# Filler weights and stores issued from GpSimd's queue, the product weights from SP's

## The chip, the cores and the metric

The kernel runs on one core of a Trainium2 chip. The metric is the device time of one execution in microseconds, the median over runs of the same program. A core has five engines that run side by side, each through its own instruction list in the order in which that list was written: TensorE (PE in the profile, its weight loads PEld), VectorE (DVE), ScalarE (ACT), GpSimd (POOL) and SyncE (SP). Transfers between HBM and the on-chip memory are started by an instruction on one of the engines' lists and then run on the DMA engines. Such an instruction waits, like any other, until its semaphores allow it, and what stands behind it on its list waits with it. "The queue" of an engine means here the DMA instructions on its list.

## The reference

Two layers (DEPTH = 2) of a hybrid mixer, on 128 context rows and 512 latent rows of width 2048. Cut to what matters here:

```python
def layer_step(x, cvec, p, rope, attend, s0_f, s0_b):
    norm_g, w_ada, b_ada, w_in, qg, kg, lb, hg, lng, lnb, ws, bs, w_out = p
    shift, scale, gate = adaln(cvec, w_ada, b_ada)      # silu(cvec) @ w_ada + b_ada, three parts of 2048
    h = rms_norm(x, norm_g) * (1.0 + scale) + shift
    aq, ak, av, ag, bq, bff, bfb, bi, bg, cu, cv, cg = split_proj(h @ w_in)   # 2048 x 6656
    q, k, v = qkv_heads(aq, ak, av, qg, kg, rope)
    a_out = attend(q, k, v) * jax.nn.silu(ag)
    b_out, s_f, s_b = hgrn_mixer(bq, bff, bfb, bi, bg, lb, hg, s0_f, s0_b)
    c_out = sgu_mixer(cu, cv, cg, lng, lnb, ws, bs)
    y = jnp.concatenate([a_out, b_out, c_out], axis=-1) @ w_out               # 2048 x 2048
    return x + gate * y, k, v, s_f, s_b
```

Outputs are the two streams after both layers, and for each layer the context's keys and values (`ck`, `cv`) and the final states of the recurrence (`st`).

## The kernel before, in words

All 640 rows (five tiles t of 128) go through the same weights. A product with `w_in` or `w_out` is made either as `rowmajor` (512 columns at a time, 16 steps k over the 2048 rows of the weight, five row tiles into five PSUM banks) or as `colmajor` (128 columns at a time, four loads of four k each). For every k, or every four k, one weight tile `wr` of 256 KB is loaded (`wraw`, line 635, pool `wrp` of 4 buffers), ACT rounds it to `wh` (line 643), DVE makes the rest `wl = wr - wh` (line 644; both in pool `whp`, 3 buffers each), and PE multiplies `wh` and `wl` with the two halves `hh` and `hl` of the activations: lines 655 to 657 (three matmuls for each of the five t, 15 for a `wr`) or line 663. In `rowmajor` the last two k share their five t.

The adaLN vectors that are not needed at once are made beside the products by a *filler*: `ada_gen` walks through blocks of 512 columns of `w_ada`, `ada_steps` makes one block. A block is 16 steps k: load a tile `wa` of 128x512 (256 KB, line 296, pool `arp` of 2 buffers), then two DVE instructions that add it, times the conditioning value of context and of latent rows, to the accumulator `aacc` (line 300 for k = 0, line 302 after it). Two more steps end a block with a few matmuls. `aacc` has one buffer. The filler gets `fill_rate` steps after each group of matmuls: 0.85 during layer 0's projections, 1.25 during its `out_proj`, 0.5 in layer 1. There are 12 blocks in layer 0 and 4 in layer 1, 256 `wa` loads in all. The first blocks of adaLN, the context projections and the first norm of layer 0 have loads of their own (`rows_block` line 264, `first_round` lines 410 and 426), which the change does not touch.

`out_proj` (line 1240 on) runs `w_out` in four passes of 512 columns, c = 0 to 3. After each pass DVE multiplies the five PSUM tiles by the gate (line 1264) and adds the residual (line 1266), and the result is stored: in layer 0 to a scratch `x1` (line 1271), in layer 1 to the outputs (line 1269). Other stores: `ck` and `cv` in `k_prep` (lines 826 and 827), `st` in `hgrn` (line 1080).

The order within an engine's list is made by a scheduler when the program is built, from the program's order, priorities and buffers that come free. A block `with self.hi():` lifts what is in it by 3000 places: loads of `wr` and `wa` are put where their buffers come free. The list of each engine is then fixed.

Of the kernel before, what the change touches and what calls it, by code (L numbers as in the profile page):

```python
# [18 lines left out]
P = 128  # L19
# [56 lines left out]
class Net:  # L76
# [213 lines left out]
    def ada_steps(self, l, blk):  # L290
        nc = self.nc
        acc = self.sml.tile([P, 2, 512], F32, tag="aacc", name=self.nm("aacc"), bufs=1)
        for k in range(KT):
            with self.hi():
                r = self.arp.tile([P, 512], F32, tag="ar", name=self.nm("wa"))
                nc.sync.dma_start(r, self.I["w_ada"][l, k * P:(k + 1) * P, 512 * blk:512 * blk + 512])
            for cd in range(2):
                sc = self.s2[:, k, cd:cd + 1]
                if k == 0:
                    nc.vector.tensor_scalar(acc[:, cd], r, sc, None, op0=ALU.mult)  # L300
                else:
                    nc.vector.scalar_tensor_tensor(acc[:, cd], r, sc, acc[:, cd], op0=ALU.mult, op1=ALU.add)  # L302
            yield
        yield
        b = self.bank()
        if blk >= 8:
            for cd in range(2):
                nc.tensor.matmul(b[32 * cd:32 * cd + 32, :], lhsT=self.ones[:, 0:32], rhs=acc[:, cd], start=True, stop=True,
                                 skip_group_check=True)
            rows = self.g(512)  # L310
            br = self.g(512)
            nc.scalar.dma_start(br[0:64], self.I["b_ada"][l, 512 * blk:512 * blk + 512].partition_broadcast(64))
            nc.vector.tensor_tensor(rows[0:64], b[0:64], br[0:64], op=ALU.add)
            c0 = 512 * (blk - 8)
            nc.scalar.dma_start(self.gd[l][:, c0:c0 + 512], rows[0:64:32])
        else:
            for i in range(4):
                for cd in range(2):
                    nc.tensor.matmul(b[:, 2 * i + cd:2 * i + cd + 1], lhsT=acc[:, cd, i * P:(i + 1) * P],  # L319
                                     rhs=self.ones[:, 0:1], start=True, stop=True, skip_group_check=True)  # L320
            self.mod_cols(l, blk // 4, 4 * (blk % 4), 4, b[:, 0:8].rearrange("p (s c) -> p s c", c=2))
        yield
# [489 lines left out]
    def k_prep(self, l):  # L812
        nc, O = self.nc, self.O
        ks = self.kss
        nc.scalar.activation(ks, ks, AF.Ln, bias=self.bias[:, 0:1], scale=1.0 / P)
        nc.scalar.activation(ks, ks, AF.Exp, scale=-0.5)
        for t in range(NT):
            kr = self.kraw[t]
            for gi in range(2):
                sl = slice(gi * P, gi * P + P)  # L820
                nc.vector.scalar_tensor_tensor(kr[:, sl], kr[:, sl], ks[:, 2 * t + gi:2 * t + gi + 1],
                                               self.gqk[:, 1], op0=ALU.mult, op1=ALU.mult)
            src = kr[:, 0:256]
            if t == 0:
                for gi in range(2):
                    nc.sync.dma_start(O["ck"][0, l, gi], kr[:, gi * P:gi * P + P])
                    nc.sync.dma_start(O["cv"][0, l, gi], self.vprm(gi))
            else:
                t1 = self.g(512)
                self.rope_ap(src, t, 2, t1[:, 0:256], t1[:, 256:512], t1[:, 0:256])  # L830
                src = t1[:, 0:256]
                yield
                yield
            b = self.bank()
            for gi in range(2):
                nc.tensor.transpose(b[:, gi * P:(gi + 1) * P], src[:, gi * P:(gi + 1) * P], self.ident)
            for gi in range(2):
                self.put_k(gi, b, None if t == 0 else self.KPOS[t])
            yield
# [211 lines left out]
    def hgrn(self, l, h, es, q):  # L1051
        nc, I, O = self.nc, self.I, self.O
# [8 lines left out]
        for d in range(2):  # L1061
            nc.sync.dma_start(S[d][:, 0], I["state_hgrn"][0, l, d, h])
            pre.append(self.hgrn_prep(l, h, d, es[d], q))
            for _ in range(8):
                yield
            kd = pre[d][5]
            kT = self.g(512)
            b = self.bank()
            for n in range(4):
                j = order[d][n]  # L1070
                nc.tensor.transpose(b[:, n * P:(n + 1) * P], kd[:, j * P:(j + 1) * P], self.ident)
            nc.scalar.activation(kT, b, AF.Copy)
            yield
            U = self.bank()
            for n in range(4):
                nc.tensor.matmul(U[:, n * P:(n + 1) * P], lhsT=kT[:, n * P:(n + 1) * P], rhs=vj[order[d][n]],
                                 start=True, stop=True, skip_group_check=True)
            So = self.sml.tile([P, P], F32, tag="So", name=self.nm("So"), bufs=2)
            nc.scalar.activation(So, U[:, 0:P], AF.Copy)
            nc.sync.dma_start(O["st"][0, l, d, h], So)  # L1080
            for n in range(1, 4):
                nc.vector.scalar_tensor_tensor(S[d][:, n], S[d][:, n - 1], pre[d][4][:, order[d][n], 4:5],
                                               U[:, n * P:(n + 1) * P], op0=ALU.mult, op1=ALU.add)
# [63 lines left out]
        for j in range(NT):  # L1147
            dst = b1[:, j * P:(j + 1) * P] if j < 4 else b2[:, 0:P]
# [90 lines left out]
    def out_proj(self, l):  # L1239
        nc, I, O = self.nc, self.I, self.O  # L1240
        last = l == DEPTH - 1
        xt = []
        for t in range(NT):
            with self.hi():
                x = self.mg()
                if l == 0:
                    src = I["x_prompt"][0] if t == 0 else I["x_sample"][0, (t - 1) * P:t * P]
                else:
                    src = self.x1[t]
                nc.scalar.dma_start(x[:, 0:D], src)  # L1250
            xt.append(x)
        ssq = self.small(4 * NT, "ssq")
        for c in range(4):
            cs = slice(512 * c, 512 * c + 512)
            gb = []
            for cd in range(2):
                gt = self.g(512)
                nc.scalar.dma_start(gt, self.gd[l][cd, cs].partition_broadcast(P))
                gb.append(gt)
            ps = self.rowmajor(I["w_out"][l], 512 * c)  # L1260
            for t in range(NT):
                with self.hi():
                    y = self.ev(512)
                    nc.vector.tensor_tensor(y, ps[t], gb[0 if t == 0 else 1], op=ALU.mult)
                xs = xt[t][:, cs]
                nc.vector.tensor_tensor(xs, xs, y, op=ALU.add)
                if last:
                    dst = O["yp"][0] if t == 0 else O["ys"][0, (t - 1) * P:t * P]
                    nc.sync.dma_start(dst[:, cs], xs)
                else:  # L1270
                    nc.sync.dma_start(self.x1[t][:, cs], xs)
                    junk = self.g(512)
                    nc.scalar.activation(junk, xs, AF.Square, accum_out=ssq[:, 4 * t + c:4 * t + c + 1])
        self.xt, self.ssq = xt, ssq
# [149 lines left out]
```

## Time and profile before

| | before |
|---|---|
| median of 3 runs | 2294.43 us (2293.33 to 2295.41) |
| the profiled execution's own time | 2299.35 us |
| its span, first to last instruction | 2297.6 us |
| mean granted TensorE clock | 0.994 |
| PE busy | 2241.8 us, 98% of the span |
| DVE, ACT, POOL busy | 1379.9, 940.4, 0.7 us |
| DMA engines' mean busy share, SP's and ACT's queues (q1 and q10 of the page are theirs) | 38.1% + 3.4% |

How to read it: a row of the waits names the engine and line that stood idle, what released it, the total in us, how often, and the longest. "SPq" is SP's list of DMA instructions. Matmuls are pipelined: a record of 0.39 us stands every 0.23 us where PE is not held up, so busy time of PE is not the same as PE at its full rate. A row of a table of windows gives, for a stretch in us from the span's start, its length, busy time and count of instructions, the granted clock, the share of the DMA engines and GB/s.

### The profile page before, as it was taken

What the parts mean: (1) busy time and instruction counts of PE and PEld (TensorE: products, weight loads), DVE (VectorE), ACT (ScalarE), POOL (GpSimd) and SP (SyncE); (2) the same over time, 40 slices, a digit from 0 to 9 for tenths busy, and PEclk for the clock granted to TensorE, in tenths of its full rate; (3) what the DMA queues carried; (4) which work ended last, traced back from release to release, by engine and by line L of the source; (5) the groups of instructions that cost most, each with busy time, mean ns of one, the idle gap of its engine ahead of it and who ended that gap; (6) DMA issues with size and microseconds to landing.
All of it is one profiled execution on the core that took longest, in us unless ns stands there. A gap on an engine that the chain in (4) does not pass through costs nothing.

```text
span 2297.6 us, 35103 instructions
## 1 busy us (share of the span) xinstructions
PE 2241.8 (98%) x13248; PEld 1943.6 (85%) x13248; DVE 1379.9 (60%) x2655; ACT 940.4 (41%) x2289; POOL 0.7 (0%) x8
## 2 busy tenths in 40 slices
PE   5999999999999999999989999999999999999999
PEld 3766678899999998978877887799999999898887
DVE  5436878648578675776668555744845644254332
ACT  4323455544554662422224246453635445233111
POOL 0000000000000000000000000000000000000000
PEclk9999999999999999999999999999999999999999
DMA  9675634334344354465553321422423322326332
GB/s 326 223 256 191 208 95 127 108 91 126 111 123 122 91 162 127 134 216 186 178 189 92 103 63 49 126 61 78 143 72 100 114 70 76 97 70 205 112 108 79
DMA packets 266031, 299.05 MB, mean 130 GB/s; under 512 B 17507, under 2 KB 166901, under 8 KB 264069
## 3 DMA queue, kind: packets, MB, share of 16 engines
q1 hardware_dynamic: 254368, 271.27, 38.1%
q10 hardware_dynamic: 11492, 25.53, 3.4%
q8 instruction: 104, 1.70, 0.3%
q14 instruction: 67, 0.54, 0.1%
HBM read 281.69 MB, written 15.04 MB: 129 GB/s over the span
## 4 chain that ended last, share of the span: by engine, by line
PE 82%; DVE 7%; DMA 6%; ACT 1%; issue 1%; DVEq 0%; SPq 0%; ACTq 0%
PE m L663 34%; PE m L655 12%; PE m L657 12%; PE m L656 12%; DMA wa<-in_w_ada_dram 5%; DVE aacc L302 2%; PE s L240 2%; PE s L898 2%; DVE wl L644 1%; PE s L944 1%; PE s L1111 1%; PE s L956 1%; PE s L1126 1%; PE s L957 1%; PE s L319 1%
## 5 line engine op out<-in xcount | busy, mean ns | idle before, releaser
L644 DVE TENSOR_TENSOR wl<-wr,wh 128x512 fp32r<-128x512 f32 (+1 forms) x535 | 367.1, 688 | 561.6 <-ACT wh L643 560.4
L643 ACT ACTIVATE wh<-wr 128x512 fp32r<-128x512 f32 (+1 forms) x535 | 336.0, 629 | 884.7 <-PE m L657 533.0
L655 PE MATMUL m<-wh,hh 128*128 128x512 f32 x1440 | 571.5, 397 | 2.7 <-ACT hh L385 2.7
L656 PE MATMUL m<-wl,hh 128*128 128x512 f32 x1440 | 568.6, 395 | 5.7 <-DVE wl L644 5.5
L657 PE MATMUL m<-wh,hl 128*128 128x512 f32 x1440 | 566.1, 394 | 0.0
L663 PE MATMUL m<-hh,wh 128*128 128x384 f32 x2016 | 477.9, 317 | 0.0
L663 PE MATMUL m<-hh,wl 128*128 128x384 f32 x2016 | 466.0, 310 | 0.0
L663 PE MATMUL m<-hl,wh 128*128 128x384 f32 x2016 | 465.8, 310 | 0.0
L302 DVE SCALAR_TENSOR_TENSOR aacc<-wa,s,aacc 128x512 f32<-128x512 f32 x480 | 344.1, 747 | 78.8 <-DMA wa<-in_w_ada_dram 77.4
L655 PEld LDWEIGHTS m<-wh,hh 128*128 128x128 f32 x1440 | 272.3, 189 | 75.4 <-issue 10.3
L656 PEld LDWEIGHTS m<-wl,hh 128*128 128x128 f32 x1440 | 272.5, 189 | 63.9 <-DVE wl L644 9.7
L657 PEld LDWEIGHTS m<-wh,hl 128*128 128x128 f32 x1440 | 272.2, 189 | 60.2 <-issue 4.7
L663 PEld LDWEIGHTS m<-hh,wh 128*128 128x128 f32 x2016 | 309.9, 188 | 14.8 <-issue 9.8
L663 PEld LDWEIGHTS m<-hh,wl 128*128 128x128 f32 x2016 | 310.0, 188 | 2.0 <-issue 1.8
L663 PEld LDWEIGHTS m<-hl,wh 128*128 128x128 f32 x2016 | 310.0, 188 | 1.9 <-issue 1.4
L1097 ACT ACTIVATE mg<-ev,Dt 128x32 f32<-128x32 f32 x480 | 113.4, 309 | 10.3 <-PE s L1111 10.1
L948 DVE TENSOR_TENSOR g<-s,g 128x512 fp32r<-128x512 f32 x56 | 38.5, 690 | 37.8 <-ACT g L947 29.9
L928 ACT ACTIVATE g<-g,st,qs 128x384 f32<-128x384 f32 (+1 forms) x64 | 48.0, 752 | 31.0 <-DVE st L924 31.0
L944 PE MATMUL s<-misc,g 128*128 128x128 f32 x240 | 45.9, 285 | 4.4 <-ACT g L933 4.0
L933 ACT ACTIVATE g<-g,st 128x384 f32<-128x384 f32 (+2 forms) x80 | 43.8, 605 | 10.9 <-DVE st L931 10.9
L898 PE MATMUL s<-kT,g 128*128 128x256 f32 (+1 forms) x288 | 46.7, 304 | 0.0
L902 DVE CUSTOM_DVE_ANT_0 g<-s,mask 128x384 f32<-128x384 f32 (+1 forms) x64 | 37.9, 622 | 13.3 <-PE s L898 13.1
(271 smaller groups left out, 1817.4 us busy)
## 6 DMA issues: line engine op xcount, KB each, us to landing
wr<-in_w_in_dram SPq DMA_DIRECT2D x406, 256.0 KB, 2.9
wa<-in_w_ada_dram SPq DMA_DIRECT2D x278, 256.0 KB, 2.9
wr<-in_w_out_dram SPq DMA_DIRECT2D x128, 256.0 KB, 3.0
wa<-in_w_ada_dram SPq DMA_DIRECT2D x16, 1024.0 KB, 6.9
wa<-in_w_in_dram SPq DMA_DIRECT2D x9, 1024.0 KB, 5.0
wa<-in_w_ada_dram SPq DMA_DIRECT2D x44, 128.0 KB, 3.6
mg<-const_xT_dram SPq DMA_DIRECT2D x4, 1280.0 KB, 5.6
x<-mg SPq DMA_DIRECT2D x20, 256.0 KB, 2.1
```

The costliest lines, as they stand in the source:

```text
L240: return self.nc.tensor.matmul(acc[32 * q:32 * q + 32, 0:n], lhsT=lhs[:, kk, :], rhs=rhs, start=kk < 4, stop=kk >= 12, skip_group_check=True)
L302: nc.vector.scalar_tensor_tensor(acc[:, cd], r, sc, acc[:, cd], op0=ALU.mult, op1=ALU.add)
L643: nc.scalar.activation(wh, raw, AF.Copy)
L644: nc.vector.tensor_tensor(wl, raw, wh.bitcast(F32), op=ALU.subtract)
L655: nc.tensor.matmul(ps, lhsT=hh, rhs=wh[:, 0], start=k == 0, stop=False)
L656: nc.tensor.matmul(ps, lhsT=hh, rhs=wl[:, 0], start=False, stop=False)
L657: nc.tensor.matmul(ps, lhsT=hl, rhs=wh[:, 0], start=False, stop=k == KT - 1)
L663: self.nc.tensor.matmul(ps[hf][:, 0:n], lhsT=w[:, a], rhs=h[:, o:o + n], start=k == 0 and i == 0, stop=k == KT - 1 and i == 2)
L898: nc.tensor.matmul(so, lhsT=x[:, hs], rhs=y[:, ks], start=i == 0, stop=i == 2, skip_group_check=True)
L928: nc.scalar.activation(dst[h], src[h], AF.Exp, bias=nmx[:, h:h + 1], scale=rq[:, h:h + 1], accum_out=den[:, h:h + 1])
L944: nc.tensor.transpose(pb[:, h * P:(h + 1) * P], dst[h][:, kb * P:(kb + 1) * P], self.ident)
L1097: nc.scalar.activation(blk[:, 4 * i + q], e[:, q], AF.Copy, scale=dd[:, i, c:c + 1])
```

## The change

Four kinds of DMA go from SP's list to GpSimd's: the 256 loads of `wa` (line 296), the 8 stores of `ck` and `cv`, the 16 of `st`, and the 40 of `x1` and the outputs. SP keeps the loads of `wr`, of the first phase and of the cached states. Sizes, buffers, priorities and arithmetic stay.

```diff
@@ ada_steps
             with self.hi():
                 r = self.arp.tile([P, 512], F32, tag="ar", name=self.nm("wa"))
-                nc.sync.dma_start(r, self.I["w_ada"][l, k * P:(k + 1) * P, 512 * blk:512 * blk + 512])
+                nc.gpsimd.dma_start(r, self.I["w_ada"][l, k * P:(k + 1) * P, 512 * blk:512 * blk + 512])
@@ k_prep
                 for gi in range(2):
-                    nc.sync.dma_start(O["ck"][0, l, gi], kr[:, gi * P:gi * P + P])
-                    nc.sync.dma_start(O["cv"][0, l, gi], self.vprm(gi))
+                    nc.gpsimd.dma_start(O["ck"][0, l, gi], kr[:, gi * P:gi * P + P])
+                    nc.gpsimd.dma_start(O["cv"][0, l, gi], self.vprm(gi))
@@ hgrn
             nc.scalar.activation(So, U[:, 0:P], AF.Copy)
-            nc.sync.dma_start(O["st"][0, l, d, h], So)
+            nc.gpsimd.dma_start(O["st"][0, l, d, h], So)
@@ out_proj
                 if last:
                     dst = O["yp"][0] if t == 0 else O["ys"][0, (t - 1) * P:t * P]
-                    nc.sync.dma_start(dst[:, cs], xs)
+                    nc.gpsimd.dma_start(dst[:, cs], xs)
                 else:
-                    nc.sync.dma_start(self.x1[t][:, cs], xs)
+                    nc.gpsimd.dma_start(self.x1[t][:, cs], xs)
```

SP's list goes from 961 rows to 644, GpSimd's from 12 to 328. Three places show what the scheduler made of it.

SP's list before, in layer 0's `out_proj`, second pass (c = 1): loads of `wa` (line 296) and of `wr` (line 635) stand in one list. The numbers behind the names tell one tile from the next.

```order
L296 DMA wa1776_10434<-in_w_ada_dram 128x512
L296 DMA wa1777_10438<-in_w_ada_dram 128x512
L635 DMA wr1795_10546<-in_w_out_dram 128x512
L296 DMA wa1781_10463<-in_w_ada_dram 128x512
L635 DMA wr1799_10571<-in_w_out_dram 128x512
L296 DMA wa1785_10488<-in_w_ada_dram 128x512
L296 DMA wa1789_10513<-in_w_ada_dram 128x512
L635 DMA wr1803_10596<-in_w_out_dram 128x512
```

GpSimd's list of the change at the same place:

```order
L296 DMA wa1776_10434<-in_w_ada_dram 128x512
L296 DMA wa1777_10438<-in_w_ada_dram 128x512
L296 DMA wa1781_10463<-in_w_ada_dram 128x512
L296 DMA wa1785_10488<-in_w_ada_dram 128x512
L296 DMA wa1789_10513<-in_w_ada_dram 128x512
```

The `wa` loads follow one another on GpSimd, and the `wr` loads of the same stretch stand alone on SP's list, in the order that they had.

DVE's list at this place, before:

```order
L302 SCALAR_TENSOR_TENSOR aacc1767_10383<-wa1781_10463,s2_115,aacc1767_10383 128x512 x2
L644 TENSOR_TENSOR wl1788_10495<-wr1786_10492,wh1787_10494 128x512
L302 SCALAR_TENSOR_TENSOR aacc1767_10383<-wa1785_10488,s2_115,aacc1767_10383 128x512 x2
L302 SCALAR_TENSOR_TENSOR aacc1767_10383<-wa1789_10513,s2_115,aacc1767_10383 128x512
L644 TENSOR_TENSOR wl1792_10520<-wr1790_10517,wh1791_10519 128x512
L302 SCALAR_TENSOR_TENSOR aacc1767_10383<-wa1789_10513,s2_115,aacc1767_10383 128x512
```

and of the change:

```order
L644 TENSOR_TENSOR wl1788_10495<-wr1786_10492,wh1787_10494 128x512
L302 SCALAR_TENSOR_TENSOR aacc1767_10383<-wa1781_10463,s2_115,aacc1767_10383 128x512
L302 SCALAR_TENSOR_TENSOR aacc1767_10383<-wa1785_10488,s2_115,aacc1767_10383 128x512 x2
L644 TENSOR_TENSOR wl1792_10520<-wr1790_10517,wh1791_10519 128x512
L302 SCALAR_TENSOR_TENSOR aacc1767_10383<-wa1789_10513,s2_115,aacc1767_10383 128x512 x2
```

A `wl` moved by one instruction against the filler's; the pattern of one or two filler steps between two `wl` is the same, and every `wl` still stands behind filler instructions that need their `wa`.

GpSimd's list at the end of that pass, where the stores of `x1` (line 1271) come in between:

```order
L296 DMA wa1831_10775<-in_w_ada_dram 128x512
L296 DMA wa1852_10839<-in_w_ada_dram 128x512
L1271 DMA x1_0_1631<-mg1667_9881 128x512
L1271 DMA x1_1_1632<-mg1668_9883 128x512
L1271 DMA x1_2_1633<-mg1669_9885 128x512
L1271 DMA x1_3_1634<-mg1670_9887 128x512
L296 DMA wa1856_10864<-in_w_ada_dram 128x512
L1271 DMA x1_4_1635<-mg1671_9889 128x512
```

Loads and stores kept the order among themselves that they had on SP's list; what left their midst are the `wr` loads.

## The prediction

> **What bounds the kernel now.** First the page's busy times, then who waited for the loads that the change separates.
>
> ```profile
> PE 2241.8 (98%) x13248; PEld 1943.6 (85%) x13248; DVE 1379.9 (60%) x2655; ACT 940.4 (41%) x2289; POOL 0.7 (0%) x8
> wr<-in_w_in_dram SPq DMA_DIRECT2D x406, 256.0 KB, 2.9
> wa<-in_w_ada_dram SPq DMA_DIRECT2D x278, 256.0 KB, 2.9
> ...
> SPq L635 <- DVE wl L644: 1157.0, 430, 15.3
> SPq L296 <- DVE aacc L302: 248.0, 210, 3.7
> ...
> L635 SPq DMA_DIRECT2D wr<-in_w_in_dram x406: 327/368/1510, 22.9 to 2048.2; - x136
> ...
>   ACT wh L643: 0.7, 1
>   PEld s L240: 0.7, 1
> ```
>
> PE is busy for 98% of the span, so only 2297.6 - 2241.8 = 55.8 us could come back at all. SP's list is nearly always waiting, but for buffers: 1157 us until DVE has read a `wr`, 248 us until it has read a `wa`. The last two rows are all that ever waited for a product weight, 1.4 us in the whole span. With four buffers `wr` is loaded long before use. So what the change gives SP, a list without `wa`, is something that nobody waits for. The filler is different; this is who waited for its loads:
>
> ```profile
> DVE aacc L302 <- DMA wa<-in_w_ada_dram: 77.4, 97, 5.3
> ...
> 1095.34 0.69 DVE L644 TENSOR_TENSOR wl<-wr,wh 128x512 fp32r<-128x512 f32 x1
> 1095.94 0.74 DVE L302 SCALAR_TENSOR_TENSOR aacc<-wa,s,aacc 128x512 f32<-128x512 f32 x1
> 1097.40 1.42 DVE L302 SCALAR_TENSOR_TENSOR aacc<-wa,s,aacc 128x512 f32<-128x512 f32 x2 [0.72 <-DMA wa<-in_w_ada_dram]
> 1098.73 0.69 DVE L644 TENSOR_TENSOR wl<-wr,wh 128x512 fp32r<-128x512 f32 x1
> 1100.04 1.42 DVE L302 SCALAR_TENSOR_TENSOR aacc<-wa,s,aacc 128x512 f32<-128x512 f32 x2 [0.62 <-DMA wa<-in_w_ada_dram]
> ...
> 1096.71 2.46 SPq L296 DMA_DIRECT2D wa<-in_w_ada_dram  x2
> ```
>
> DVE waits for `wa` 97 times. The timeline of layer 0's `out_proj` shows a ring: the two instructions of a step end at about 1096.7, SP issues the next load into that buffer at 1096.71, without delay, and DVE uses it at 1100.04, 3.3 us later, having waited for it. With two buffers in the ring, two steps take one such turn. SP's list does not hold `wa` up here; the transfer's own 2.9 us does. And `wl`, which PE needs, stands behind these waits on DVE.
>
> How far `wl` is ahead of PE decides what a longer turn costs. Where it is not ahead, PE waits already; the rows are of the stretches 988.5 to 1020.5 and 1160.2 to 1182.6 (first and last pass):
>
> ```profile
> DVE aacc L302 <- DMA wa<-in_w_ada_dram: 8.0, 5, 3.7
> PEld m L656 <- DVE wl L644: 7.7, 6, 2.9
> PE m L656 <- DVE wl L644: 5.0, 4, 2.5
> ...
> DVE aacc L302 <- DMA wa<-in_w_ada_dram: 5.1, 7, 1.0
> PEld m L656 <- DVE wl L644: 2.0, 4, 1.0
> ```
>
> Elsewhere I paired each `wl` with the first L656 that reads it, by counting (five a tile, 80 a pass), at the point in each burst where the distance is least:
>
> ```profile
> 1068.16 1.41 DVE L644 TENSOR_TENSOR wl<-wr,wh 128x512 fp32r<-128x512 f32 x2
> 1071.64 0.39 PE L656 MATMUL m<-wl,hh 128*128 128x512 f32 x1
> ...
> 1121.84 0.69 DVE L644 TENSOR_TENSOR wl<-wr,wh 128x512 fp32r<-128x512 f32 x1
> 1124.48 0.39 PE L656 MATMUL m<-wl,hh 128*128 128x512 f32 x1
> ...
> 908.57 0.69 DVE L644 TENSOR_TENSOR wl<-wr,wh 128x512 fp32r<-128x512 f32 x1
> 909.62 0.39 PE L656 MATMUL m<-wl,hh 128*128 128x512 f32 x1
> ...
> 1268.82 0.69 DVE L644 TENSOR_TENSOR wl<-wr,wh 128x512 fp32r<-128x512 f32 x1
> 1270.55 0.39 PE L656 MATMUL m<-wl,hh 128*128 128x512 f32 x1
> ```
>
> The leads are 1071.64 - 1068.85 = 2.8 us (the first of the two), 1124.48 - 1122.53 = 2.0, 909.62 - 909.26 = 0.4, and 1270.55 - 1269.51 = 1.0. The whole kernel is bound by PE, but in these bursts the ring of `wa` eats PE's lead.
>
> **The change part by part.** *What a `wa` load costs from GpSimd.* No DMA of the trace is issued there, so the price d, by which a load lands later after its buffer comes free, has to be bounded.
>
> ```profile
> L296 SPq DMA_DIRECT2D wa<-in_w_ada_dram x256: 327/328/691, 196.1 to 1799.2; - x128
> L216 POOL MEMSET att<- 128x128 f32 x2 | 0.4, 206 | 0.0
> L215 POOL MEMSET tp<- 128x25 f32 x2 | 0.2, 121 | 0.3 <-POOLq L1400 0.3
> ```
>
> From below: if preparing the transfer costs nothing on GpSimd, SP's 0.33 us falls away, d = -0.33. From above: SP's slowest issue of a load, L635's 1.51 us quoted above, is 1.2 over its 0.33, d = +1.2. I take +0.8, nearer to the upper end, because of the only rows that GpSimd has: from 25 to 128 elements a memset grows by 85 ns, 0.83 ns an element on top of 0.1. If it works through a tile's 128 rows with, as I assume, four words for the read and four for the write of each, that is 1024 x 0.83 + 100 = 0.95 us, 0.6 more than SP's 0.33, and I add 0.2 for starting it, where SP starts without delay. The Trainium skill ("DMA: Bandwidth & Descriptors", Latency and other measured facts) gives the first byte after about 1 us from GpSimd's path against 0.6 from SP's; an estimate by that page is d = 0.4, and the sum below would come to +8 us instead of +25. No run here shows it yet.
>
> *What it costs PE.* Two buffers share a turn, so each pair of steps takes d longer. The steps in each burst, two L302 a step:
>
> ```profile
> 988.50:1020.50 32.00, 15.45 (x22) 0.98 0.60 195
> 1036.00:1068.50 32.50, 19.95 (x28) 1.00 0.61 191
> 1091.00:1123.70 32.70, 19.34 (x28) 1.00 0.61 195
> 1160.20:1182.60 22.40, 14.10 (x20) 1.00 0.57 184
> 889.00:916.00 27.00, 15.99 (x23) 1.00 0.61 180
> 1250.00:1271.00 21.00, 13.53 (x19) 1.00 0.59 178
> ```
>
> That is 5.5, 7, 7, 5, 5.75 and 4.75 pairs. At d = 0.8, less the lead: first pass 4.4; second 5.6 - 2.8 = 2.8; third 5.6 - 2.0 = 3.6; fourth 4.0; the block around 900 us 4.6 - 0.4 = 4.2; the block around 1260 us 3.8 - 1.0 = 2.8. Together 21.8 us. DVE has time left overall (60% busy), but it is behind within a burst, and PE cannot win back what it has waited.
>
> *The other blocks.* They lie beside attention and the recurrence, where the lead is larger; the least that I found:
>
> ```profile
> 1800.41 0.69 DVE L644 TENSOR_TENSOR wl<-wr,wh 128x512 fp32r<-128x512 f32 x1
> 1804.40 0.45 PE L663 MATMUL m<-hh,wl 128*128 128x384 f32 x2
> ```
>
> 1804.40 - 1801.10 = 3.3 us; their loads are waited for less often. Of the 97 waits the six bursts have 5, 11, 12, 7, 6 and 7 (by the same view of each; the row of the fourth is shown), so about 49 are here. If all came onto the path, 49 x 0.8 = 39 us; if the lead hides all, nothing. I take 3, since PE's list also has attention's matmuls, which wait for DVE without buffers between.
>
> *The stores.* Nobody waits for `ck`, `cv`, `st` and the outputs; `x1` is read again only in layer 1. The very last five stores end the span, and there d counts once: 0.8. Stores stand among the `wa` loads as before (the list shows it), so they block them no more than they did.
>
> *SP's list without `wa`.* Only where the first phase's own loads still share SP's list can `wa` come sooner, up to some 230 us. What PE idles there at the end:
>
> ```profile
> 172.30:229.80 57.50, 54.93 (x272) 38.38 (x273) 35.67 (x78) 19.24 (x33) 0.00 (x0) 1.00 0.59 191
> ```
>
> At most 57.50 - 54.93 = 2.6 us could come back; I take 1, as PE needs none of the filler's results there.
>
> Sum: 21.8 + 3 + 0.8 - 1 = +24.6 us, on the profiled execution's 2299.35 that is 2324. The runs' median is 4.9 lower than that execution; on it, 2294.43 + 24.6 = **2319 us**.
>
> With d = 1.2 the bursts give 6.6 + 5.6 + 6.4 + 6.0 + 6.5 + 4.7 = 36, the other blocks perhaps a quarter of 49 x 1.2, 15, the end 1.2: +52, 2346.
>
> **The rivals.** *No change that can be measured* (0.2%, 4.6 us, is about what a measurement of this kernel can tell from none): d of 0.3 or less. Then the first and fourth pass lose 1.7 + 1.5, the block at 900 1.3, the one at 1260 0.4, the others nothing, the start gives 1 back: +4, 2298. For it: the issue itself is only 0.33 of 2.9 us. Against it: it needs GpSimd to be almost as quick as the hardware path.
>
> *Faster*: the ring turns faster from GpSimd, the point being d below 0. At d = -0.33 the first pass wins 1.8, the fourth 1.7, the end 0.3 and the start all of its 2.6: -6.4, 2288. For it: GpSimd has nothing else to do (0.7 us busy). Against: SP issues a `wa` at once after its buffer is free, so there is no queueing to win, and product weights were waited for 1.4 us in all.
>
> *Slower by far: DVE keeps GpSimd from preparing transfers.* In these bursts DVE starts its next instruction just when a buffer comes free; were GpSimd held off until that one has ended, another 0.75 us (L302) would come on d: 1.55. Bursts 8.5 + 8.0 + 8.8 + 7.8 + 8.5 + 6.4 = 48, a third of 49 x 1.55 in the others, 25, the end 1.6: +74, 2369. The trace speaks neither for nor against it, since GpSimd did nothing then. The Trainium skill ("SBUF — State Buffer", Who interferes with whom) says that GpSimd's transfers starve only beside DVE instructions in a two-port mode, not beside ones like L302 and L644 with two inputs; by that rule this rival fails, and only L300, two in 32 here, would count.
>
> **How the numbers follow.** The forecast (d from 0.35 to 1.3, slower) has 58%, held off by DVE 10%, no difference 20%, faster 12%. Slower by over 0.2% thus 0.68, within 0.20, faster 0.12. The forecast's own range is 2300 to 2350; with most of the other cases, 2291 to 2357.
>
> **What would show it.** In the profile after: `wr` still waited for about 1 us; the `wa` loads of GpSimd land about 3.7 us after issue counted from the free buffer; DVE's wait for `wa` grows from 77 to some 120 us (97 waits, about half of them first of a pair, by 0.8); PE's waits L656 <- DVE `wl` appear in the second and third pass, where there are none, and grow in the first and fourth; granted clock unchanged outside these. I am wrong if `wa` lands as soon as before (then no change), if DVE's waits grow and PE's don't (then the lead was larger than I paired it), or if PE loses most beside attention and the recurrence.

## The result, and the profile after

The change makes the kernel slower: median of 4 runs 2349.87 us (2348.64 to 2356.42) against 2294.92 us (2293.33 to 2298.37) of the kernel before on the same chip, a ratio of 1.0242 with a 95% interval of 1.0230 to 1.0254. That is +55 us where +24.6 were forecast. The profiled execution took 2356.42 us with a span of 2354.6, 57 more than the span before.

The page of the changed kernel: busy times, and the row of the `wa` loads among its DMA issues (the last number is the median time from issue to landing). Then, of its table of waits, the rows that answer to those shown before (total us, times, longest):

```profile
PE 2253.5 (96%) x13248; PEld 1948.1 (83%) x13248; DVE 1380.6 (59%) x2655; ACT 939.7 (40%) x2289; POOL 174.7 (7%) x328
wa<-in_w_ada_dram POOLq DMA_DIRECT2D x256, 256.0 KB, 3.2
...
DVE aacc L302 <- DMA wa<-in_w_ada_dram: 142.8, 125, 5.7
...
PEld m L656 <- DVE wl L644: 26.4, 17, 4.4
...
PE m L656 <- DVE wl L644: 19.2, 17, 3.9
...
PE s L1111 <- DVE mg L1082: 8.9, 2, 5.3
...
PEld s L240 <- DMA wr<-in_w_in_dram: 1.0, 2, 0.7
```

DVE waits for `wa` 143 us instead of 77, and PE for DVE's `wl` 19 instead of 5.5. A wait that was 1.3 us in all before, L1111 for DVE's L1082, is now 8.9: the recurrence. Product weights were and are waited for about 1 us. The busy time of PE holds a second loss: the same 13248 instructions are busy 2253.5 - 2241.8 = 11.7 us longer. Their clock was halved more often (mean granted clock 0.989 instead of 0.994): PE was busy during 35.5 us of the halved stretches instead of 21.0, and half of that is 17.7 us instead of 10.5. So 7.2 of the 11.7 us are matmuls at half clock. At least a part of the rest comes with the stands themselves, since a record of 0.39 us that the next one would have overlapped after 0.23 counts in full before a stand. Of the 57.0 us that the span grew, 45.3 are time without any matmul, 7.4 of these behind PE's last one.

Where the time went can be read from PE, by the start of the same matmul in both traces (the first L656 or L663 with `wl` of each pass). Times on the left are those of the kernel before:

| stretch before, us | lost, us | my term |
|---|---|---|
| 0 to 280, first phase and context projections | 7.7 | -1 |
| 280 to 487, beside attention | 5.8 | "other blocks", 3 in all |
| 487 to 841, beside the recurrence | 14.1 | (the same 3) |
| 841 to 963, block around 900 | 1.9 | 4.2 |
| 963 to 1213, the four passes of `out_proj` | 16.2 | 4.4 + 2.8 + 3.6 + 4.0 = 14.8 |
| 1213 to 1410, block around 1260 | 3.3 | 2.8 |
| 1410 to the last matmul | 0.7 | (the same 3) |
| behind the last matmul | 7.4 | 0.8 |

How one late `wa` becomes 5.6 us shows at one place in the recurrence. First the kernel before: DVE's timeline, PE's row at L1111, and windows around it (length, busy times with counts, then the granted clock, the DMA share and GB/s):

```profile
740.89 1.41 DVE L302 SCALAR_TENSOR_TENSOR aacc<-wa,s,aacc 128x512 f32<-128x512 f32 x2
743.42 1.42 DVE L302 SCALAR_TENSOR_TENSOR aacc<-wa,s,aacc 128x512 f32<-128x512 f32 x2 [1.11 <-DMA wa<-in_w_ada_dram]
...
747.92 1.42 DVE L302 SCALAR_TENSOR_TENSOR aacc<-wa,s,aacc 128x512 f32<-128x512 f32 x2 [1.04 <-DMA wa<-in_w_ada_dram]
749.25 0.72 DVE L1082 SCALAR_TENSOR_TENSOR mg<-mg,EG,s 128x128 f32<-128x128 f32 x2
749.89 0.68 DVE L644 TENSOR_TENSOR wl<-wr,wh 128x512 fp32r<-128x512 f32 x1
750.49 0.34 DVE L1082 SCALAR_TENSOR_TENSOR mg<-mg,EG,s 128x128 f32<-128x128 f32 x1
...
750.98 0.42 PE L1111 MATMUL s<-mg,g 128*32 128x128 f32 x8 [1.26 <-DVE mg L1082]
...
753.00:763.00 10.00, 10.00 (x82) 8.71 (x81) 3.81 (x10) 8.97 (x36) 0.00 (x0) 1.00 0.29 82
```

The same place in the changed kernel, with GpSimd's timeline (a number in brackets is the idle time before it and what ended it):

```profile
764.78 0.75 DVE L302 SCALAR_TENSOR_TENSOR aacc<-wa,s,aacc 128x512 f32<-128x512 f32 x1 [1.07 <-DMA wa<-in_w_ada_dram]
765.45 0.68 DVE L644 TENSOR_TENSOR wl<-wr,wh 128x512 fp32r<-128x512 f32 x1
766.05 0.74 DVE L302 SCALAR_TENSOR_TENSOR aacc<-wa,s,aacc 128x512 f32<-128x512 f32 x1
767.46 1.41 DVE L302 SCALAR_TENSOR_TENSOR aacc<-wa,s,aacc 128x512 f32<-128x512 f32 x2 [0.66 <-DMA wa<-in_w_ada_dram]
768.79 0.72 DVE L1082 SCALAR_TENSOR_TENSOR mg<-mg,EG,s 128x128 f32<-128x128 f32 x2
770.43 0.75 DVE L302 SCALAR_TENSOR_TENSOR aacc<-wa,s,aacc 128x512 f32<-128x512 f32 x1 [0.92 <-DMA wa<-in_w_ada_dram]
771.10 0.68 DVE L644 TENSOR_TENSOR wl<-wr,wh 128x512 fp32r<-128x512 f32 x1
771.70 0.34 DVE L1082 SCALAR_TENSOR_TENSOR mg<-mg,EG,s 128x128 f32<-128x128 f32 x1
...
767.10 0.54 POOL L296 DMA_DIRECT2D wa<-in_w_ada_dram  x1 [2.55 <-DVE aacc L302]
...
772.19 0.65 PE L1111 MATMUL s<-mg,g 128*32 128x128 f32 x8 [5.30 <-DVE mg L1082]
...
770.00:780.00 10.00, 7.81 (x62) 6.07 (x62) 6.18 (x15) 5.17 (x19) 1.32 (x3) 0.71 0.48 138
```

The last of three L1082, for which PE stands, comes behind filler instructions that wait; one of them (770.43) even stands between the three, where before only a `wl` did. PE's stand grows from 1.26 to 5.30 us, and right after it the clock of a 10 us window is 0.71 where it was 1.00. A clock of one half over 2 x 0.29 x 10 = 5.8 us makes that 0.71; 2.2 us of them are still the stand, and the other 3.6 cost the matmuls 1.8. With the longer stand, 5.30 - 1.26 = 4.0, that is 5.8 us; by the starts of the same matmuls, this pass lost 5.6. The Trainium skill ("TensorE: Matmul & The Clock Gate", Part 1) has the clock at one half after an idle window of about 3.4 us, in windows that run freely. The halved stretches here are whole multiples of 3.4 us (6.8 at this place), but stands of 1.97 and 1.81 us, shorter than a window, were enough for one each; here the measurement decides.

The ring's turn can be read from the same rows. Before, a buffer is free at 740.89 + 1.41 = 742.30 and one at 743.42 + 1.42 = 744.84; the use of the second's next tile begins at 747.92, 3.08 us later, after a wait. In the changed kernel one is free at 766.05 + 0.74 = 766.79, GpSimd begins to issue at 767.10, and the use begins at 770.43, 3.64 us later. Over all loads the shortest turn is 2.73 us before and 3.33 after. So the price d is 0.6 us: 0.3 until GpSimd begins, 0.3 because the tile lands 3.2 instead of 2.9 us after its issue.

### The profile page after: what moved, and what is told of

Same layout as the page of the kernel before. It is cut to its first block, busy times and chain, and to the rows that moved or that the text cites. A ratio compares the mean times of both kernels' runs of the same rounds, so it can differ in the third digit from the quotient of the medians.

```text
span 2354.6 us, 35226 instructions
## 1 busy us (share of the span) xinstructions
PE 2253.5 (96%) x13248; PEld 1948.1 (83%) x13248; DVE 1380.6 (59%) x2655; ACT 939.7 (40%) x2289; POOL 174.7 (7%) x328
## 4 chain that ended last, share of the span: by engine, by line
issue 47%; PE 29%; DMA 15%; DVE 6%; ACT 1%; POOL 1%; POOLq 0%; SPq 0%; DVEq 0%; ACTq 0%
PE m L663 14%; DMA wa<-in_w_ada_dram 13%; PE m L655 3%; PE m L656 3%; PE m L657 3%; DVE aacc L302 3%; PE s L240 2%; DVE wl L644 1%; PE s L1111 1%; DMA mg<-const_xT_dram 1%; PE s L663 1%; PE s L898 1%; POOL out_dram L1269 0%; DVE ev L1264 0%; DVE mg L1266 0%
## 5 line engine op out<-in xcount | busy, mean ns | idle before, releaser
L644 DVE TENSOR_TENSOR wl<-wr,wh 128x512 fp32r<-128x512 f32 (+1 forms) x535 | 366.4, 687 | 558.3 <-ACT wh L643 552.3
L656 PE MATMUL m<-wl,hh 128*128 128x512 f32 x1440 | 569.9, 396 | 19.2 <-DVE wl L644 19.2
L663 PE MATMUL m<-hh,wh 128*128 128x384 f32 x2016 | 479.7, 318 | 0.9 <-DVE ev L1162 0.9
L663 PE MATMUL m<-hh,wl 128*128 128x384 f32 x2016 | 468.5, 311 | 0.0
L663 PE MATMUL m<-hl,wh 128*128 128x384 f32 x2016 | 467.2, 311 | 0.0
L302 DVE SCALAR_TENSOR_TENSOR aacc<-wa,s,aacc 128x512 f32<-128x512 f32 x480 | 345.0, 746 | 144.3 <-DMA wa<-in_w_ada_dram 142.8
L656 PEld LDWEIGHTS m<-wl,hh 128*128 128x128 f32 x1440 | 272.7, 189 | 81.2 <-DVE wl L644 26.4
L663 PEld LDWEIGHTS m<-hh,wh 128*128 128x128 f32 x2016 | 311.4, 189 | 16.4 <-issue 10.2
L663 PEld LDWEIGHTS m<-hh,wl 128*128 128x128 f32 x2016 | 312.0, 189 | 2.2 <-issue 1.8
L663 PEld LDWEIGHTS m<-hl,wh 128*128 128x128 f32 x2016 | 311.3, 189 | 1.8 <-issue 1.6
L296 POOL DMA_DIRECT2D wa<-in_w_ada_dram x256 | 139.2, 544 | 1574.6 <-DVE aacc L302 572.9
L944 PE MATMUL s<-misc,g 128*128 128x128 f32 x240 | 45.3, 282 | 5.1 <-ACT g L933 4.9
```

The costliest lines, as they stand in the source:

```text
L296: nc.gpsimd.dma_start(r, self.I["w_ada"][l, k * P:(k + 1) * P, 512 * blk:512 * blk + 512])
L644: nc.vector.tensor_tensor(wl, raw, wh.bitcast(F32), op=ALU.subtract)
L656: nc.tensor.matmul(ps, lhsT=hh, rhs=wl[:, 0], start=False, stop=False)
L663: self.nc.tensor.matmul(ps[hf][:, 0:n], lhsT=w[:, a], rhs=h[:, o:o + n], start=k == 0 and i == 0, stop=k == KT - 1 and i == 2)
```

## The experiments

All were timed against the kernel before on the same chip (medians between 2291.8 and 2296.1 us there). A ratio is to that kernel.

### Loads alone, stores alone

```diff
# loads alone: the stores (826, 827, 1080, 1269, 1271) back on SP
-                nc.gpsimd.dma_start(dst...)
+                nc.sync.dma_start(dst...)
# stores alone: the loads (296) back on SP
-                nc.gpsimd.dma_start(r, self.I["w_ada"]...)
+                nc.sync.dma_start(r, self.I["w_ada"]...)
```

> Only the 256 loads of wa go to GpSimd's queue; all stores stay on SP's. Theory A (each wa load lands about 0.6 us later, DVE is late with wl and with the small tiles of attention and the recurrence, PE stands and its clock is halved for a while after the longer stands): nearly the whole loss but the end's, 55 - 7 = +48, about 2343 us; GpSimd has long been done at the end. Rival D (stores on GpSimd's list hold up the loads behind them): the loads alone lose much less, below +40, under 2335. If the stores gave nothing and cost nothing, end included: 2350.

Measured: 2342.02 us, ratio 1.0203 (1.0181 to 1.0226), +47.

> Only the 64 stores go to GpSimd's queue; the loads of wa stay on SP's. Theory C (after its last stores GpSimd closes its list with a drain of about 9.5 us, for which the end of the program waits): about +7, 2302 us, all of it behind PE's last matmul, and the span's end 11 to 12 us behind PE's end instead of 4.6. Rival (the end costs one later landing, as I had predicted): +0.8, 2295.7. Rival D (stores matter to loads): something changes before PE's last matmul as well.

Measured: 2302.13 us, ratio 1.0030 (1.0019 to 1.0040), +6.8. The two add up to the change within 2 us (47 + 6.8 against 55), so the stores do not hold the loads up; that rival fell. The end was expected 11 to 12 us behind PE's last matmul; with the stores alone it lies 8.4 us behind it, where it was 4.6 in the kernel before. So the trace places 3.8 of the 6.8 us there, and the other 3 are not located. What the stores do at the end shows in the rows of GpSimd's closing instructions (count, duration in ns min/median/max, first and last start in us), of the kernel before, the changed one, stores alone and loads alone:

```profile
L1413 POOLq DRAIN  x3: 34/78/452, 0.8 to 2297.3; - x3
```
```profile
L1413 POOLq DRAIN  x3: 40/102/9456, 2344.4 to 2354.4; - x3
```
```profile
L1413 POOLq DRAIN  x3: 45/102/5859, 2292.9 to 2299.3; - x3
```
```profile
L1413 POOLq DRAIN  x3: 40/102/4901, 1847.7 to 2343.0; - x3
```

Behind its last transfer GpSimd's list closes with a drain of 4.9 to 9.5 us. Where the last transfer is the last output store, the program's end waits for it; with the loads alone it lies at 1847.7 us and nobody does.

### The last stores back on SP

```diff
-                    nc.gpsimd.dma_start(dst[:, cs], xs)
+                    nc.sync.dma_start(dst[:, cs], xs)
```

> The changed kernel with only the 20 stores of the last layer's outputs back on SP's queue. Theory C (the drain of GpSimd after its own last transfer is what the end waits for): that drain, whatever its length, now lies beside PE's work, and the end is 4.6 us behind PE's again: 2350 - 7 = 2343 us. Rival (a drain of 9.5 us comes at the end of the program wherever GpSimd's last transfer lies, or the landing itself is slow): still 2349 or more.

Measured: 2344.43 us, ratio 1.0211 (1.0194 to 1.0228). PE's last matmul and the end are 5.2 us apart instead of 12.0; a drain of 7.8 us lies at 1971 us, beside PE's work. As expected.

### The filler's first block on SP

```diff
-                nc.gpsimd.dma_start(r, ...)
+                (nc.sync if (l, blk) == (0, 8) else nc.gpsimd).dma_start(r, ...)
```

> The changed kernel with the loads of the filler's first block alone (16 of 256, about 200 to 313 us) on SP's queue. Theory A: in that block one of the two buffers still belongs to the context projections, every step takes a whole turn, and the 7.1 us that were lost between 204 and 280 us go; the rest stays: 2343 us, with 280 us reached within 1 us of the kernel before. Rival (stores of ck and cv on GpSimd's list, or the traffic of its path, delay the start): 2349.

Measured: 2347.70 us, ratio 1.0228 (1.0213 to 1.0244): not to be told from the changed kernel, whose interval overlaps. In the trace the point 280 us is reached 0.8 us late instead of 7.7, but the runs with the loads alone and with the last stores on SP, which have that block on GpSimd, are 3.9 and 5.0 late there. So the first block costs some 4 us, and how much of it reaches the end is not settled.

### Three buffers for `wa`

```diff
-        self.wrp = ec(tc.tile_pool(name="wrp", bufs=4))
+        self.wrp = ec(tc.tile_pool(name="wrp", bufs=3))
-        self.arp = ec(tc.tile_pool(name="arp", bufs=2))
+        self.arp = ec(tc.tile_pool(name="arp", bufs=3))
```

> The changed kernel with three buffers for wa instead of two, the room taken from wr (three instead of four). Theory A (the turn of the ring is the cause): three steps share a turn of 3.6 us, 1.2 us for each, less than the 1.4 us of DVE's two instructions, so DVE's waits for wa mostly go (from 143 us to under 50) and with them the PE stands before the end: 2295 + 7 for the end = 2302 us, perhaps below. Rival B (the new order of the lists, or traffic of the GpSimd path itself, costs PE): the loss stays, 2340 or more. If the fourth buffer of wr was needed, PE's and ACT's waits for wr (1 us now) grow.

> The kernel before with three buffers for wa and three for wr, everything on SP's queue. It is the control of the run with three buffers on GpSimd's queue, and a candidate to beat both. Theory A: the ring already cost the kernel before something (PE's and PEld's waits for wl 15 us, and 24 us at half clock): 2280 to 2290 us. Between this and the same with GpSimd's queue only the end remains, about 7 us. Rival: with one buffer less, wr comes late: PE or ACT wait for wr by more than 10 us, and it is slower than before.

Measured: 2346.71 us (ratio 1.0220, 1.0203 to 1.0237) on GpSimd's queue and 2304.26 (1.0035, 1.0022 to 1.0048) on SP's. Both missed. The reason lies in the first phase; the row of PE's wait there, in the kernel before, on GpSimd's queue and on SP's:

```profile
PE s L371 <- DVE g L369: 14.4, 1, 14.4
```
```profile
PE s L371 <- DVE g L369: 52.1, 1, 52.1
```
```profile
PE s L371 <- DVE g L369: 32.5, 1, 32.5
```

The free third buffer let the filler begin at once, with its DVE instructions among those that PE needs first. From 280 us on the two kernels gained 10 and 18 us on the kernel before (the next expectation counts from 204 us). So both were repeated with the third buffer held by a tile of zeros until the context projections:

```diff
+        self.held = self.padded()
-        nc.vector.tensor_copy(shp[:, :, 0:2], self.sh[:, 0])
+        nc.vector.tensor_tensor(shp[:, :, 0:2], self.sh[:, 0], self.held[:, :, 0:2], op=ALU.add)
```

> The kernel before with three buffers for wa and three for wr; unlike the first run of this kind, the third buffer of wa is held by a tile of zeros until the context projections begin, so that the filler starts at its old place and not ahead of the first phase. Theory A (the ring's turn): the first kernel with three buffers on SP's queue won 14 us against before from 280 us on and lost 19 ahead of it; without that loss 2281 us, give or take 5 for the buffer that wr gives up. If it stays at 2300 or more, the missing buffer of wr is what costs, and not the filler's early start.

> The same three buffers with the filler at its old place, and the queues of the changed kernel (wa and all stores on GpSimd's). Theory A: with three buffers a step needs 3.6 / 3 = 1.2 us of the ring, less than DVE's 1.4 for its two instructions, so a landing that is 0.6 us later costs PE nearly nothing: as the same on SP's queue, plus 4 for what DVE's waits still do, plus 7 for the drain at the end: 2292 us, 50 to 58 below the changed kernel. Rival B (GpSimd's queue costs PE something that has nothing to do with the number of buffers): 2325 or more.

Measured: 2290.62 us on SP's queue (ratio 0.9976, 0.9966 to 0.9985) and 2310.00 on GpSimd's (1.0067, 1.0052 to 1.0082). DVE's wait, GpSimd's queue first, then SP's (L303 is L302 here):

```profile
DVE aacc L303 <- DMA wa<-in_w_ada_dram: 36.7, 48, 4.4
```
```profile
DVE aacc L303 <- DMA wa<-in_w_ada_dram: 20.2, 19, 4.2
...
ACT wh L644 <- DMA wr<-in_w_in_dram: 15.6, 4, 8.9
```

With two buffers the two queues are 55 us apart, with three 19, and 7.4 of these are the end (here too 12.0 us behind the last matmul). So with three buffers GpSimd's queue costs PE 12 us; if it costs no more than that as such, the ring of two costs the rest. Both missed their expectations. SP's version was expected at 2281: with three buffers `wr` comes late in the first 280 us, where it loses 8. GpSimd's was expected at 2292, 11 us above SP's, and came 19 above it.

### Later landing without GpSimd

Two transfers for a `wa`, on SP's and on GpSimd's queue, and four on SP's:

```diff
-                nc.sync.dma_start(r, ...[512 * blk:512 * blk + 512])
+                for q in range(2):
+                    nc.sync.dma_start(r[:, 256 * q:256 * q + 256], ...[512 * blk + 256 * q:512 * blk + 256 * q + 256])
```

> The kernel before, everything on SP's queue, each wa loaded by two transfers of 128x256 instead of one of 128x512. SP's second issue follows 0.33 us after the first, so the tile should be complete about 0.3 us later, with GpSimd taking no part. Theory A (what costs is when wa lands, whichever engine issues it): 48 us for 0.58 us, so about 25 for 0.3 us, 2320 us, between 2305 and 2325; stands of PE in the same places as in the changed kernel, but shorter. Rival B (GpSimd's queue as such is the cause): within 5 us of 2295.

> The changed kernel with each wa loaded by two transfers of 128x256, both from GpSimd. If GpSimd prepares each in the 0.54 us that one of 128x512 took, since both have 128 rows, the tile lands about 0.5 us later again, 1.1 us later than from SP. Theory A, in proportion: 48 more, about 2395 us, the drain at the end no shorter than 9.5 us. If the loss does not grow in proportion (PE's lead is used up, so each further 0.1 us counts in full): up to 2420. Rival B (the cause is not when wa lands): within 10 us of 2350.

Measured: 2292.41 us (ratio 0.9985, 0.9976 to 0.9994) and 2352.62 (1.0247, 1.0231 to 1.0263). Both missed, since the landing did not do what I had expected: with halves on SP the shortest turn is 2.61 us, not longer but 0.12 shorter than with one transfer, and on GpSimd 3.18 instead of 3.33. The row of the halves on SP (issues; then time to landing):

```profile
L297 SPq DMA_DIRECT2D wa<-in_w_ada_dram x512: 327/420/2118, 196.2 to 1792.9; - x171
...
DMA to landing us min/median/max: 2.0/2.3/5.3
```

By the medians a half lands 2.3 us after its issue, a whole 2.9. The Trainium skill ("Perfetto Trace Analysis", DMA Optimizations) says that a split may let a task end sooner where the DMA engines are mostly idle; here it does, by that 0.12. These two runs thus tested nothing about a later landing. On GpSimd's queue the 0.15 us won nothing (+56.6 where whole loads cost 55); why is open. Quarters do land later:

> The kernel before, everything on SP's queue, each wa loaded by four transfers of 128x128. With two halves the second issue stood 0.38 us behind the first and the half landed about 2.2 us after its issue; with four the last issue stands 1.13 behind the first, so the tile is complete about 3.3 us after its buffer is free, against 2.7 at the least in the kernel before: 0.5 to 0.6 us later, as from GpSimd (3.3), and GpSimd takes no part. Theory A (what costs is when wa lands): close to the changed kernel without its end, 2335 us, between 2320 and 2350, with the same stands of PE before L656, L1076 and L1111. Rival B (GpSimd's queue as such costs PE): 2295, within 5.

Measured: 2292.94 us, ratio 0.9992 (0.9982 to 1.0001). The shortest turn is 3.32 us, as from GpSimd, and nothing is lost. So a landing that is 0.6 us later does not by itself cost 48 us: my theory in that form fell, and the rival "GpSimd's queue as such" stood again. But DVE's list had changed too. At the place shown above it now reads (L1083 is L1082, L645 is L644):

```profile
743.60 1.42 DVE L303 SCALAR_TENSOR_TENSOR aacc<-wa,s,aacc 128x512 f32<-128x512 f32 x2 [0.16 <-DMA wa<-in_w_ada_dram]
745.33 1.11 DVE L1083 SCALAR_TENSOR_TENSOR mg<-mg,EG,s 128x128 f32<-128x128 f32 x3 [0.31 <-ACT So L1080]
746.36 0.69 DVE L645 TENSOR_TENSOR wl<-wr,wh 128x512 fp32r<-128x512 f32 x1
```

No filler instruction stands among the three. When the kernel was built with quarters, the scheduler put the filler later: 398 of its 512 instructions have another place among the `wl`, on the mean 1.5 `wl` further back. With the loads on GpSimd it moved only 82, by 0.1 on the mean. Between the last use of a buffer and its next use DVE has at most 2.25 us of other work 93 times before, 90 times in the changed kernel, and 40 times with quarters. Why the scheduler moved the filler is not shown; that it took the four transfers for a later tile is my guess.

### Queue and list crossed

So I pinned the filler's places among the `wl` of one kernel to those of another (`PLACE` holds them):

```diff
+    def pin(self):
+        def after(b, a):
+            self.tc.add_manual_dep(b, a.name, mybir.DependencyInfo(mybir.DependencyClass.NoSync, mybir.DependencyReason.DATA),
+                                   reason="issue order")
+        j = 0
+        for acc, step in zip(self.accs, PLACE.split()):
+            j += int(step)
+            after(acc, self.wls[j])
+            after(self.wls[j + 1], acc)
```

> The changed kernel, queues and all, but with the place of each filler instruction among DVE's wl (L644) pinned to that of the run with quarters on SP's queue, where tiles landed as late and nothing was lost. In that list DVE has 2.2 us or less of other work between the last use of a wa buffer and its next use 39 times, in the changed kernel's own list 88 times. Theory E (a landing that is 0.6 us later costs only where DVE's list puts the next use close behind, and the changed kernel's list was laid out as if the tile came as early as before): DVE's wait for wa falls from 143 to about 95 us and nearly all of the loss before the end goes: 2296 + 7 for the end = 2303 us, between 2297 and 2312. Theory A without the order (0.6 us later is the loss, whatever the list) or B (GpSimd's queue as such): 2340 or more.

> The other corner: everything on SP's queue, wa in quarters (landing 0.6 us later), but each filler instruction pinned among DVE's wl to its place in the changed kernel's list. Theory E: the loss comes back without GpSimd, less what the rest of the list has loosened: DVE's wait for wa 115 to 140 us, 2330 us, between 2312 and 2343. If it stays at 2293, the order among filler and wl is not what spared the run with quarters, and what did is open.

> The kernel before, whole wa loads on SP's queue (the early landing), with each filler instruction pinned among DVE's wl to its place in the changed kernel's list. Those two lists differ in 82 of 512 places. Theory E (late landing and a tight list together): no loss without the late landing, 2295, within 6, DVE's wait for wa 70 to 85 us. If the changed kernel's list is worse by itself, or pinning costs by itself, it is slower than 2305, and then the same part of the two crossed runs is not the landing's.

> The kernel before, whole wa loads on SP's queue, with the filler's places in DVE's list pinned to those of the run with quarters, which put the filler 1.5 wl later on the mean. It is the control of GpSimd's queue with this list (2319). Theory E: early landing and a loose list: at most before's time, 2288 to 2295, DVE's wait for wa under 50 us; between it and GpSimd's queue with the same list stand 7 for the end, about 5 for the first block and little else. If pinning this list into another kernel costs by itself, it costs here too, above 2300.

Medians, and their difference to the kernel before on the same chip:

| loads of `wa`, shortest turn | the changed kernel's list | the list of the quarters |
|---|---|---|
| whole, SP, 2.7 us | 2294.75 (-1.1; ratio 0.9983 to 1.0001) | 2299.48 (+3.7; 1.0002 to 1.0021) |
| whole, GpSimd, 3.3 us | 2349.87 (+55.0, 7.4 of them the end) | 2318.64 (+26.8, 7.4 the end; 1.0096 to 1.0127) |
| quarters, SP, 3.3 us | 2365.01 (+73.2; 1.0296 to 1.0330) | 2292.94 (-2.6) |

DVE's wait for `wa` in the four pinned kernels, in the order of their expectations (L314 and L315 are L302):

```profile
DVE aacc L314 <- DMA wa<-in_w_ada_dram: 70.4, 69, 4.5
```
```profile
DVE aacc L315 <- DMA wa<-in_w_ada_dram: 125.8, 91, 6.4
```
```profile
DVE aacc L314 <- DMA wa<-in_w_ada_dram: 87.9, 100, 4.8
```
```profile
DVE aacc L314 <- DMA wa<-in_w_ada_dram: 39.9, 44, 4.2
```

The list alone costs nothing (-1.1, though DVE waits 88 us, a little over the 85 expected), the late landing alone costs nothing (-2.6), both together cost 48 us on GpSimd's queue and 73 on SP's, where GpSimd takes no part. So the cause of most of the loss is the late landing and the tight list together, whichever engine issues. One limit remains: only the filler's places among the `wl` are the same within a column of the table; DVE's other work was placed anew in each build. The sizes were missed twice. The quarters with the changed kernel's list lost 73, not 35: 23 us of them between 1213 and 1277 us of the kernel before and 12 between 859 and 916. PE stood there for other DVE work, while DVE's own waits for `wa` come to 5.3 and 7.4 us only; that the pinning put this work late is inferred. That leaves 38 us of the 73. PE's longest waits in the two stretches (L849 and L1212 are lines 836 and 1199 before):

```profile
PE s L849 <- DVE g L767: 5.6, 3, 2.0
...
PE s L1212 <- DVE ev L1198: 7.5, 2, 4.2
```

GpSimd with the loose list lost 27, not 11. Of that, 10.9 us lie at 1213 to 1277, and the same list loses 12.1 there with whole loads on SP, so that piece is the pinning's, and it is also why that control is 3.7 us slower and not faster, as I had expected. By the differences in the table GpSimd's queue costs 26.8 - 3.7 = 23.1 us with the loose list, 7.4 of it the end, and 55.0 + 1.1 = 56.1 with the tight one. The rest with the loose list was not expected either: in the traces 8.7 us of it lie in the four passes of `out_proj`, where the control wins 9.1 us on the kernel before and GpSimd's queue 0.3. So where the filler is densest, the late landing still takes away what the loose list wins.

### A version that beats both

Three buffers for `wa` held back as above, all on SP's queue, four buffers for `wr`, and the room taken from the large working tiles (`gp`, six instead of seven); then the same with halves.

> Three buffers for wa, the filler at its old place, everything on SP's queue as in the kernel before; the room comes from the pool of large working tiles (six instead of seven), and wr keeps its four. With wr at three buffers the first 280 us lost 8 us and the rest won 16. Theory: without that loss 2295 - 14 = 2281 us. If the working tiles are short in attention and the recurrence, it loses there instead, and is no faster than 2290.

> Three buffers for wa with the filler at its old place, six large working tiles, wr with four buffers, all on SP's queue, and each wa in two transfers of 128x256. With two buffers the halves won 4 us, since the two together landed about 0.1 us sooner than the whole. Theory A: with three buffers DVE waits for wa 19 us only, against 77, so little of that is left to win: 2286, between 2283 and 2288, on the 2287 of the same without halves. If halves help in another way as well, they win their 4 us again: 2283.

Measured: 2287.42 us, ratio 0.9961 (0.9948 to 0.9973), 8.7 us under the kernel before, and 2291.57, ratio 0.9977 (0.9968 to 0.9986) with halves. The first is the fastest kernel of this study, though it was expected at 2281. With three buffers halves win nothing (they were expected at 2286), which fits that what they won with two was the ring's. Whether they lose anything is open, as the two intervals overlap.

## Why the prediction was right or wrong, point by point

The direction and the mechanism held, the size did not: +55 against +24.6. The traces lost 57.1 us, 32.5 more than the sum: 17.6 in "the other blocks", 8.7 at the start, 6.6 at the end, and 0.4 less in the bursts. The step that failed is first of all the term of 3 us for the other blocks.

- **SP's list has nothing to gain.** Right: product weights were waited for 1 us before and after.
- **The price d.** Taken as 0.8, measured as 0.6: the issue takes 0.54 us, not the 0.95 worked out from the memsets, but GpSimd begins after 0.3 us, not 0.2. The estimate by the Trainium skill ("DMA: Bandwidth & Descriptors", Latency and other measured facts) of 0.4 was as near; the measurement lies between.
- **DVE's waits.** 120 us expected, 143 measured.
- **The six bursts.** 21.8 us expected, 1.9 + 16.2 + 3.3 = 21.4 measured. This agreement is luck. At d = 0.6 my own terms give 3.3 + 1.4 + 2.2 + 3.0 + 3.1 + 1.9 = 14.9, and pass by pass the four of `out_proj` lost 0.8, 8.5, 1.8 and 5.1 us where the terms were 4.4, 2.8, 3.6 and 4.0. The lead was paired rightly, but pairs times d, less the least lead, does not give what a pass loses; what does is open. The halved clock does not make up the difference: in these stretches it cost 7.2 us before and 6.4 after.
- **"The other blocks", 3 us.** This step failed: 5.8 + 14.1 + 0.7 = 20.6. I looked for the least lead of a `wl`, 3.3 us, and took PE's other matmuls as nearly free. But L1111 waits for a single small DVE tile with no lead at all, and so do, by way of ACT, L1076 and attention's L944: before the stand of 3.38 us at L1076, ACT's list had waited 5.64 us for a DVE tile (L227) that stood behind a waiting filler instruction. I had written that attention's "wait for DVE without buffers between", and still took 3 of a possible 39. Here also lay the sign that I had set: I should be wrong "if PE loses most beside attention and the recurrence". It loses as much there as in the bursts.
- **The granted clock "unchanged".** Wrong: 7.2 of the 57 us are matmuls at half clock, behind the first phase each time after PE stood for 1.8 us or more.
- **The start, -1.** Wrong sign, 4 to 8 us lost in the traces. One of the two buffers still belongs to the context projections there, so every step takes a whole turn; I used that stretch only to bound a gain.
- **The end, 0.8.** Wrong: 7.4. I counted a landing and not what GpSimd does after its last transfer; no row of the trace before had a transfer of GpSimd, so this could have been bounded only from other kernels.
- **The rival "DVE keeps GpSimd from preparing transfers"** fell. GpSimd's issue of a `wa` takes 0.54 us nearly all through, with DVE 59% busy; 6 of the 256 take over 0.56:

```profile
L296 POOL DMA_DIRECT2D wa<-in_w_ada_dram x256: 536/538/833, 197.0 to 1850.3; - x128
```

  The Trainium skill's rule ("SBUF — State Buffer", Who interferes with whom), by which DVE instructions like L302 and L644 do not starve it, agrees with this row. "No change" and "faster" fell with d.
- **What no step said.** I took DVE's list as given and saw that it hardly moved. That it did not move was the harm: the list suited tiles that come 0.6 us sooner. With the list of the quarters, where the filler stands further back, the same lateness was free on SP's queue.

## What to carry to other kernels

When a load is moved to a slower path, look at who stands behind its consumer in the consumer's own list: here a landing 0.6 us later was free where the list had other work in that gap, and where it had not, PE stood, at times with a halved clock on top. The scheduler kept nearly the old list here (82 of 512 places moved); a third buffer brought the loss down from 55 to 15 us, a looser list to 27. Keep an output store at the very end off GpSimd's queue, or let its last transfer come early.

## What was not expected of the hardware

- GpSimd closes with a drain after its last transfer: 4.9, 5.9, 7.8, 9.5 and 4.4 us in five kernels with 256, 64, 300, 320 and (halves) 576 transfers on its list, so not in proportion to their number. What sets its length is open.
- From GpSimd a 128x512 tile is issued in 0.54 us, 0.3 us after its buffer is free, where SP needs 0.33 and begins at once; it lands 0.6 us later in all.
- By the shortest turns, all on SP, two transfers of half a tile were complete 0.12 us before one of the whole (2.61 against 2.73 us), four quarters 0.59 after it.
- In the changed kernel, stands of TensorE of 1.81 and 1.97 us were followed by a stretch of 3.4 us at half clock; others of 1.4 to 1.9 us were not, nor was one of 2.2 us in the control with the quarters' list.
